# A new head, a middle without rstd and one weight unit split by hand in a decoder layer kernel

## The chip, the cores and the metric

One Trainium2 chip, one of its cores. The metric is the device time of one execution in microseconds (us). The core has the engines TensorE (PE), VectorE (DVE), ScalarE (ACT), GpSimd (POOL) and SyncE (SP); in this kernel SP issues the weight transfers and waits for nothing else that matters here.

## The reference

One layer of a decoder on x (256 rows of 1024 channels, float32), cut to what the kernel's parts need:

```
h   = rmsnorm(x, norm_mix)
o_a, o_b, o_c = attention mixers on columns of h @ w_in      # dilated, sparse, block-sparse
g   = sigmoid(the last 3 * 1024 columns of h @ w_in)          # one gate per branch and channel
merged = g0 * (o_a @ wb[:r0]) + g1 * (o_b @ wb[r0:r1]) + g2 * (o_c @ wb[r1:])
x   = x + merged @ w_out
a,u = split(causal_conv3(rmsnorm(x, norm_ffn) @ w_up) + conv_b)   # 2 * 2816 columns
x   = x + (silu(a) * u) @ w_down
out = rmsnorm(x, norm_final)       # rmsnorm(y, w) = y * rsqrt(mean(y*y) + 1e-6) * w
```

The convolution is depthwise over the 256 rows: for each channel, `w2 * y[t] + w1 * y[t-1] + w0 * y[t-2]`.

## The kernel before

Every weight matrix is stored as units, most of them 128x2048 float32 (1 MB). SP's queue loads a unit into a `raw` tile; ACT copies it to `whi`, rounded to the type that PE multiplies at its full rate (L225), and DVE takes the rest, `wlo = raw - whi` (L229), each in two halves of 128x1024. `raw`, `whi` and `wlo` sit in rings of five slots. An activation is split likewise (`hn_hi`, `hn_lo`; `mh`, `ml`; `fh`, `fl`), and a product is three matmuls into one PSUM tile: whi·lo, wlo·hi and whi·hi (`mm3`, L241 to L243; the weight is named first here). PE, ACT, DVE and POOL each run their own instructions in order; a scheduler sets that order, except inside a `manual_schedule` block, where it is the order of the code. The stages:

- Head. rstd of x's rows (ACT square L170, DVE L177/L179, POOL power L181), x scaled by it (L282, L290, L291), eight transposes per row tile through an identity matrix that came by DMA in `small_a` (L275), then parts hi (L302, L304) and lo (L307) with the norm weights as a per-partition scale. Idle matmuls (`keep_busy`, L262) fill PE. The first unit `a0` is multiplied chunk by chunk in the order of L337: hi·hi, lo·hi, hi·wlo; the next unit is `a1`.
- Projections and attention, up to 161 us, untouched by the change.
- Merge, four rounds `i` of two chunks `c`. A chunk has 24 products `g` with unit `br{i}` (three branches), DVE gates and adds them (`mg`: L713, L715 `tmp`, L716), ACT and DVE split the sum (`mh` L719, `ml` L720), and 12 matmuls of 128x512 with unit `wo{i}` go into four `acc` tiles. `later` holds these 12 back by a chunk or two; `flush` emits the last 24 of them. In round 1 `wlo` of the `br` unit is made on POOL instead of DVE (L697).
- Middle. x gets the residual (`add`, L735), then its rstd (`square`, POOL power), is scaled by rstd and by `norm_ffn` in one DVE instruction (`scale`, L742), transposed (`turned`, L748), split (`turn_hi` L752, `turn_lo` L756); four idle matmuls stand ahead (L774).
- MLP, 11 iterations of units `fa`, `fu`, `fd`, two channel chunks each. A chunk is 24 products with `fa`, 24 with `fu`, and 12 `acc` matmuls with `fd`. `conv` reads the PSUM tile three times: ACT L800, then DVE L802 twice; silu on ACT (L822), the product `sa` (L824), the split `fh` (L827) and `fl` (L828) follow.
- Final norm and store.

Of the kernel before, what the change touches and what calls it, by code (L numbers as in the profile page):

```python
# [32 lines left out]
A_ID, A_GM, A_N = 0, 128, 136  # L33
# [4 lines left out]
def _constants():  # L38
# [27 lines left out]
    return np.eye(P, dtype=np.float32), sel, mk, onehot, mask  # L66
# [36 lines left out]
def _laid_out(a):  # L103
# [3 lines left out]
    for name, src, rows, cols in _unit_list():  # L107
# [7 lines left out]
    eye, sel, mk, onehot, mask = _constants()  # L115
# [3 lines left out]
    small_a = np.concatenate([eye, turn(a["norm_mix"])], 1)  # L119
# [3 lines left out]
    return dict(x=a["x"][0], small_a=small_a, small_b=small_b, table=table, w1=w1, wts=wts,  # L123
                norms=np.stack([a["norm_ffn"][0], a["norm_final"]]))
# [3 lines left out]
def decoder_layer(ctx: ExitStack, tc, x, small_a, small_b, table, w1, wts, norms, out):  # L128
# [11 lines left out]
    xs = act_pool.tile([P, NT, D], F32, name="xs")  # L140
    sa_ = const.tile([P, A_N], F32, name="small_a")
# [8 lines left out]
    ident, g_mix = sa_[:, A_ID:A_ID + P], sa_[:, A_GM:A_GM + KC]  # L150
# [119 lines left out]
    u_a0 = Unit("a0", cuts=2)  # L270
    HALF = [slice(n * 512, (n + 1) * 512) for n in range(2)]
# [5 lines left out]
    with tc.manual_schedule(engines={mybir.EngineType.Activation, mybir.EngineType.DVE, mybir.EngineType.Pool,  # L277
                                     mybir.EngineType.PE}):
        keep_busy(WARM)
        r = rstd_of([square_mean(xs[:, 0, :], xn[0], "m0")], "m0")  # L280
        for sl in HALF:
            nc.vector.tensor_scalar_mul(xn[0][:, sl], xs[:, 0, sl], r)  # L282
        turn(0)
        keep_busy(2)
# [13 lines left out]
        u_a0.lo(0, 2, nc.gpsimd)  # L298
# [65 lines left out]
    for i in range(3):  # L364
# [4 lines left out]
        else:  # L369
            u = unit(f"a{i}")  # L370
# [313 lines left out]
    def flush(t):  # L684
        for n in range(2):
            for e in waiting:
                e(t, n)
        if t == NT - 1:
            waiting.clear()
# [43 lines left out]
    xn = [act_pool.tile([P, D], F32, name=f"xn{t}") for t in range(NT)]  # L733
# [3 lines left out]
    def square(t, n):  # L737
        return square_mean(xs[:, t, HALF[n]], xn[t][:, HALF[n]], f"f{t}{n}")

    def scale(t, r, n):  # L740
        for sl in HALF[n:n + 1]:
            nc.vector.scalar_tensor_tensor(xn[t][:, sl], xs[:, t, sl], r, g_ffn[:, sl], op0=ALU.mult, op1=ALU.mult)  # L742

    def turned(t, n):
        pool, name = ((psg, "g"), (psg2, "g"), (psa, "acc00"), (psa, "acc01"))[2 * t + n]
        ps = pool.tile([P, 512], F32, name=name).rearrange("p (c q) -> p c q", c=4)
        for c in range(4):
            nc.tensor.transpose(ps[:, c, :], xn[t][:, (4 * n + c) * P:(4 * n + c + 1) * P], ident)  # L748
        return ps

    def turn_hi(t, n, ps):
        nc.scalar.activation(h_hi[:, 4 * n:4 * n + 4, t * P:(t + 1) * P], ps, AF.Copy)  # L752

    def turn_lo(t, n, ps):
        hi = h_hi[:, 4 * n:4 * n + 4, t * P:(t + 1) * P]
        nc.vector.tensor_sub(h_lo[:, 4 * n:4 * n + 4, t * P:(t + 1) * P], ps, hi.bitcast(F32))  # L756

    fu = dict(first)
    with tc.manual_schedule(engines={mybir.EngineType.Activation, mybir.EngineType.DVE, mybir.EngineType.Pool}):
        flush(0)  # L760
        flush(1)
        add(0, 0)
        s00 = square(0, 0)
        add(0, 1)
        s01 = square(0, 1)
# [103 lines left out]
```

## Time and profile before

| what | value |
|---|---|
| three timed executions | 445.3, 445.21, 443.75 us, median 445.21 us |
| the profiled execution, its own time | 445.4 us |
| its span, first to last instruction | 443.6 us |
| mean granted TensorE clock | 0.991 |
| busy PE / DVE / ACT / POOL | 97% / 67% / 54% / 4% |

The span leaves 1.8 us of the execution's time to what lies around it. A busy time is the part of the span in which an engine had at least one instruction at work. The granted clock is a share of PE's full clock: 1.0 is 2.4 GHz, 0.5 is 1.2 GHz.

### The profile page before, as it was taken

Reading aid. Unit: us, or ns where it says so; the run is one execution under the profiler, and the core shown is the slowest. Engines: PE = TensorE matmul, PEld = TensorE weight load, DVE = VectorE, ACT = ScalarE, POOL = GpSimd, SP = SyncE. Lnnn points to the kernel's source line nnn. Section 1 sums busy time; section 2 is a strip of 40 time slices with the busy share of each in tenths; the row PEclk is TensorE's granted clock in tenths of the full one; section 3 lists DMA queues with packets and bytes.
Section 4 is the critical chain, followed back from the end, with each engine's and each line's share of the span. In section 5 each row is a group of like instructions: output and inputs, shape, how many; then the busy total and the mean of one; then the engine's idle time right before and its main releaser. Section 6 shows DMA issues by size and latency. Waiting matters only on the chain.

```text
span 443.6 us, 7635 instructions
## 1 busy us (share of the span) xinstructions
PE 430.0 (97%) x3094; PEld 391.2 (88%) x3094; DVE 295.5 (67%) x593; ACT 240.3 (54%) x420; POOL 17.8 (4%) x20
## 2 busy tenths in 40 slices
PE   7999999999999998999999899999999999999993
PEld 6998877977789996999998799999999999999982
DVE  4846742888466487646535998785785785875744
ACT  4643362558676772445442795465564573574423
POOL 2401000000000031000000100000000000000001
PEclk9999999999999998999999999999999999999997
DMA  8978746331127795345550177743733734700002
GB/s 305 395 287 277 262 166 258 136 150 41 57 95 269 270 364 190 128 157 191 189 191 1 61 278 279 284 154 131 285 134 151 286 104 181 264 22 1 1 0 95
DMA packets 12898, 78.66 MB, mean 177 GB/s; under 512 B 1424, under 2 KB 1568, under 8 KB 4928
## 3 DMA queue, kind: packets, MB, share of 16 engines
q1 hardware_dynamic: 12144, 76.00, 45.9%
q0 software_dynamic: 576, 2.12, 1.7%
q8 instruction: 24, 0.39, 0.4%
q10 hardware_dynamic: 144, 0.07, 0.1%
q14 instruction: 10, 0.08, 0.1%
HBM read 77.11 MB, written 1.07 MB: 176 GB/s over the span
## 4 chain that ended last, share of the span: by engine, by line
PE 92%; DVE 3%; ACT 2%; issue 1%; DMA 1%; POOL 1%; POOLq 0%; DVEq 0%
PE g L243 21%; PE g L241 21%; PE g L242 21%; PE acc L241 6%; PE acc L242 6%; PE acc L243 6%; PE s L428 3%; PE o L460 2%; PE g L337 2%; PE t L439 2%; PE o L522 1%; DMA xs<-in_x_dram 1%; DVE mg L716 1%; PE s L337 1%; ACT whi L225 0%
## 5 line engine op out<-in xcount | busy, mean ns | idle before, releaser
L229 DVE TENSOR_TENSOR wlo<-raw,whi 128x1024 fp32r<-128x1024 f32 (+2 forms) x132 | 151.5, 1177 | 54.8 <-ACT whi L225 53.7
L241 PE MATMUL g<-hn_hi,wlo 128*128 128x256 f32 x648 | 185.1, 286 | 0.0
L242 PE MATMUL g<-hn_lo,whi 128*128 128x256 f32 x648 | 184.4, 285 | 0.0
L243 PE MATMUL g<-hn_hi,whi 128*128 128x256 f32 x648 | 184.4, 285 | 0.0
L225 ACT ACTIVATE whi<-raw 128x1024 fp32r<-128x1024 f32 (+2 forms) x136 | 131.9, 1014 | 28.6 <-PE g L243 17.1
L241 PEld LDWEIGHTS g<-hn_hi,wlo 128*128 128x128 f32 x648 | 124.1, 192 | 3.8 <-issue 2.3
L242 PEld LDWEIGHTS g<-hn_lo,whi 128*128 128x128 f32 x648 | 124.1, 192 | 2.7 <-issue 1.9
L243 PEld LDWEIGHTS g<-hn_hi,whi 128*128 128x128 f32 x648 | 124.1, 192 | 1.3 <-issue 1.3
L802 DVE SCALAR_TENSOR_TENSOR cy<-g,small_b,cy 128x255 f32<-128x255 f32 (+1 forms) x88 | 42.0, 481 | 26.5 <-ACT cy L800 25.3
L800 ACT ACTIVATE cy<-g,small_b 128x256 f32<-128x256 f32 x44 | 24.8, 566 | 23.8 <-PE g L243 22.4
L241 PE MATMUL acc<-whi,fl 128*128 128x512 f32 x88 | 34.5, 393 | 0.0
L242 PE MATMUL acc<-wlo,fh 128*128 128x512 f32 x88 | 34.5, 392 | 0.0
L243 PE MATMUL acc<-whi,fh 128*128 128x512 f32 x88 | 34.3, 389 | 0.0
L827 ACT ACTIVATE fh<-sa 128x256 fp32r<-128x256 f32 x22 | 9.2, 417 | 34.7 <-DVE sa L824 34.7
L639 ACT ACTIVATE gl<-g 128x256 f32<-128x256 f32 x24 | 9.1, 381 | 23.6 <-PE g L243 23.6
L243 PEld LDWEIGHTS acc<-whi,fh 128*128 128x128 f32 x88 | 16.5, 188 | 3.6
L241 PEld LDWEIGHTS acc<-whi,fl 128*128 128x128 f32 x88 | 16.6, 189 | 3.0
L242 PEld LDWEIGHTS acc<-wlo,fh 128*128 128x128 f32 x88 | 16.6, 189 | 2.8
L242 PE MATMUL g<-o_lo,whi 128*128 128x256 f32 x64 | 18.1, 283 | 0.0
L243 PE MATMUL g<-o_hi,whi 128*128 128x256 f32 x64 | 18.1, 283 | 0.0
L241 PE MATMUL g<-o_hi,wlo 128*128 128x256 f32 x64 | 18.1, 283 | 0.0
L476 ACT ACTIVATE tt<-tt,nm 128x128 f32<-128x128 f32 (+1 forms) x32 | 14.3, 448 | 4.9 <-DVE nm L474 4.8
(176 smaller groups left out, 490.4 us busy)
## 6 DMA issues: line engine op xcount, KB each, us to landing
raw<-in_wts_dram SPq DMA_DIRECT2D x62, 1024.0 KB, 4.8
gl<-in_w_dram SPq DMA_DIRECT2D x8, 512.0 KB, 6.7
raw<-in_wts_dram SPq DMA_DIRECT2D x2, 804.0 KB, 8.0
raw<-in_wts_dram SPq DMA_DIRECT2D x3, 512.0 KB, 6.9
T<-tvd POOLq DMA_DIRECT2D x1, 1280.0 KB, 12.9
xs<-in_x_dram SPq DMA_DIRECT2D x2, 512.0 KB, 4.3
g<-in_norms_dram SPq DMA_DIRECT2D x2, 512.0 KB, 4.0
out_dram<-raw SPq DMA_DIRECT2D x4, 256.0 KB, 2.2
```

Of the source, the lines that this page charges most:

```text
L225: nc.scalar.activation(self.parts[0][:, sl], self.raw[:, sl], AF.Copy)
L229: (eng or nc.vector).tensor_sub(self.parts[1][:, sl], self.raw[:, sl], self.parts[0][:, sl].bitcast(F32))
L241: nc.tensor.matmul(ps, al, bh, start=start, stop=False)
L242: nc.tensor.matmul(ps, ah, bl, start=False, stop=False)
L243: nc.tensor.matmul(ps, ah, bh, start=False, stop=stop)
L337: nc.tensor.matmul(ps, view(a, k), b[:, k, :], start=(a == 0 and b is h_hi and k == 0), stop=(a == 1 and k == KC - 1))
L428: nc.tensor.matmul(pss[i][:, o], q[rows, q0:q0 + P], k[rows, 0:k1], start=True, stop=True)
L476: nc.scalar.activation(t[:, a:b], t[:, a:b], AF.Exp, bias=nm[:, i:i + 1], accum_out=z[:, i:i + 1])
L639: nc.scalar.activation(gl[c][:, b, :], chunk_T(plain(u, c)), AF.Copy)
L800: nc.scalar.activation(y, ps, AF.Identity, bias=vec_c[:, 3, ch:ch + 1], scale=vec_c[:, 2, ch:ch + 1])
L802: nc.vector.scalar_tensor_tensor(y[:, sh:], ps[:, :S - sh], vec_c[:, w, ch:ch + 1], y[:, sh:], op0=ALU.mult, op1=ALU.add)
L827: nc.scalar.activation(fh, sa, AF.Copy)
```

## The change

Four parts. (1) The head makes the identity on POOL, finds `norm_mix` and `norm_ffn` as eight further columns of x's rows, takes 16 idle matmuls of 128x128 in place of six of 128x256 and drops the later ones, computes both rstd before any scaling, shares the scaling and the split of `a0` differently, splits `a1` by hand, and orders the products of the first chunk hi·hi, then by halves of k. (2) `wlo` of `br1` is made on DVE. (3) In the middle x is transposed as it is, and `norm_ffn` enters in the split; the products of `fa0` and `fu0` are written out by hand with `fu0` split between them; rstd comes later, as a row (`rows`, two small fp32 matmuls). The idle matmuls go. (4) `conv` multiplies the PSUM tile by `rows` on DVE first (`u`) and works on `u` in SBUF. The core of the diff:

```
-WARM = 6
+WARM = 16
...
-    nc.scalar.dma_start(sa_, small_a)
+    g_mix, g_ffn = xs[:, 0, D:D + KC], xs[:, 1, D:D + KC]
...
+    nc.gpsimd.affine_select(out=ident, in_=idle, compare_op=ALU.not_equal, fill=1.0, base=0, pattern=[[-1, P]],
+                            channel_multiplier=1)
...
-        keep_busy(WARM)
-        r = rstd_of([square_mean(xs[:, 0, :], xn[0], "m0")], "m0")
-        for sl in HALF:
-            nc.vector.tensor_scalar_mul(xn[0][:, sl], xs[:, 0, sl], r)
-        turn(0)
-        keep_busy(2)
...
+        for _ in range(WARM):
+            nc.tensor.matmul(pt[:, :P], idle, idle, start=True, stop=True)
+        r0 = rstd_of([square_mean(xs[:, 0, 0:D], xn[0], "m0")], "m0")
...
+        scaled(0, 0, r0, "v")
+        scaled(0, 1, r0, "a")
+        turn(0)
+        scaled(1, 0, r1, "v")
+        scaled(1, 1, r1, "a")
         turn(1)
-        u_a0.hi(0, 2)
-        keep_busy(1)
...
+        split_hi(0, "v")
+        split_hi(1, "a")
+        u_a0.lo(0, 2, nc.gpsimd)
+        for c in (0, 1):
+            hi_part(c, "v")
+        for c in (2, 3):
+            hi_part(c, "a")
+        split_hi(2, "a")
+        split_hi(3, "a")
+        u_a0.lo(1, 2, nc.gpsimd)
+        for c in range(4, KC):
+            hi_part(c, "v")
+        for i in range(2):
+            u_a1.hi(i, 2)
+        for c in range(KC):
             lo_part(c)
+        for i in range(2):
+            u_a1.lo(i, 2)
...
-        u = unit(f"br{i}", eng=nc.gpsimd if i == 1 else None)
+        u = unit(f"br{i}")
...
+def turn_hi(c):
+        nc.scalar.activation(h_hi[:, c, :], xT[c], AF.Copy, scale=g_ffn[:, c:c + 1])
...
+        for t in range(NT):
+            flush(t, 0)
+            add(t, 0)
+            sq[t, 0] = square(t, 0)
+        flush(0, 1)
         add(0, 1)
+        xT += turned(0)
+        flush(1, 1)
...
+        split_x(0)
         add(1, 1)
+        split_x(2)
+        first_products(0, h_hi, range(4))
+        u_f.lo(0, 2)
+        xT += turned(1)
+        first_products(0, h_lo, range(4))
+        split_x(4)
+        split_x(6)
+        first_products(0, h_hi, range(4, KC))
+        u_f.lo(1, 2)
+        for t in range(NT):
+            sq[t, 1] = square(t, 1)
+        rs = [rstd_of([sq[t, 0], sq[t, 1]], f"f{t}") for t in range(NT)]
+        fu["fa1"] = unit("fa1")
+        first_products(0, h_lo, range(4, KC))
+
+        rp = psa.tile([P, 512], F32, name="acc00")[:, :S]
+        for t in range(NT):
+            nc.tensor.matmul(rp[:, t * P:(t + 1) * P], rs[t].to_broadcast([P, P]), ident, start=True, stop=True)
+        nc.scalar.activation(rows, rp, AF.Copy)
...
-        nc.scalar.activation(y, ps, AF.Identity, bias=vec_c[:, 3, ch:ch + 1], scale=vec_c[:, 2, ch:ch + 1])
+        u = scaled.pop(0)
+        scaled.append(u)
+        nc.vector.tensor_mul(u, ps, rows)
+        nc.scalar.activation(y, u, AF.Identity, bias=vec_c[:, 3, ch:ch + 1], scale=vec_c[:, 2, ch:ch + 1])
         for w, sh in ((1, 1), (0, 2)):
-            nc.vector.scalar_tensor_tensor(y[:, sh:], ps[:, :S - sh], vec_c[:, w, ch:ch + 1], y[:, sh:],
+            nc.vector.scalar_tensor_tensor(y[:, sh:], u[:, :S - sh], vec_c[:, w, ch:ch + 1], y[:, sh:],
```

`split_x(c0)` makes the hi parts of two chunks of x on ACT and then their lo parts on DVE; `first_products(part, b, ks)` multiplies one part of both units by one part of x into four PSUM tiles. The lines of the diff move instructions on the queues; three places follow.

DVE in the first merge round, before. `mg_1956` is the gated sum of round 0, chunk 0, `mg_1995` that of chunk 1, `ml_1991` the lo part that the first 12 `acc` matmuls need, and `wlo_2227` belongs to unit `wo1`.

```order
L713 TENSOR_TENSOR mg_1956<-g_1958,gl_1549 128x256
L715 TENSOR_TENSOR tmp_1957<-g_1969,gl_1549 128x256
L716 TENSOR_TENSOR mg_1956<-mg_1956,tmp_1957 128x256
L715 TENSOR_TENSOR tmp_1957<-g_1981,gl_1549 128x256
L716 TENSOR_TENSOR mg_1956<-mg_1956,tmp_1957 128x256
L713 TENSOR_TENSOR mg_1995<-g_1997,gl_1550 128x256
L720 TENSOR_TENSOR ml_1991<-mg_1956,mh_1990 128x256
```

The same place after the change; `mg_1967`, `mg_2006` and `ml_2002` are the same three, `wlo_2058` is `br1`'s lo part, `wlo_2238` that of `wo1`.

```order
L725 TENSOR_TENSOR mg_1967<-g_1969,gl_1560 128x256
L227 TENSOR_TENSOR wlo_2058<-raw_2056,whi_2057 128x1024
L727 TENSOR_TENSOR tmp_1968<-g_1980,gl_1560 128x256
L227 TENSOR_TENSOR wlo_2058<-raw_2056,whi_2057 128x1024
L728 TENSOR_TENSOR mg_1967<-mg_1967,tmp_1968 128x256
L725 TENSOR_TENSOR mg_2006<-g_2008,gl_1561 128x256
L727 TENSOR_TENSOR tmp_1968<-g_1992,gl_1560 128x256
L727 TENSOR_TENSOR tmp_2007<-g_2019,gl_1561 128x256
L728 TENSOR_TENSOR mg_1967<-mg_1967,tmp_1968 128x256
L728 TENSOR_TENSOR mg_2006<-mg_2006,tmp_2007 128x256
L727 TENSOR_TENSOR tmp_2007<-g_2031,gl_1561 128x256
L227 TENSOR_TENSOR wlo_2238<-raw_2236,whi_2237 128x1024
L732 TENSOR_TENSOR ml_2002<-mg_1967,mh_2001 128x256
```

Two halves of `br1` moved in among chunk 0's adds, a half of `wo1` moved ahead of `ml`, and `ml` comes after the multiplications of chunk 1.

PE at the same place, before: the last product of chunk 1 (`g_2020`) and the first `acc` matmuls.

```order
L241 MATMUL g_2020<-o_hi_84,wlo_1941 128x256
L242 MATMUL g_2020<-o_lo_85,whi_1940 128x256
L243 MATMUL g_2020<-o_hi_84,whi_1940 128x256
L241 MATMUL acc00_1935<-whi_1948,ml_1991 128x512
L242 MATMUL acc00_1935<-wlo_1949,mh_1990 128x512
L243 MATMUL acc00_1935<-whi_1948,mh_1990 128x512
```

After, the last rows before the first `acc` matmul; `g_2098` is the third branch of round 1, chunk 0.

```order
L239 MATMUL g_2098<-o_hi_83,wlo_2058 128x256
L240 MATMUL g_2098<-o_lo_84,whi_2057 128x256
L241 MATMUL g_2098<-o_hi_83,whi_2057 128x256
L239 MATMUL g_2098<-o_hi_83,wlo_2058 128x256
L240 MATMUL g_2098<-o_lo_84,whi_2057 128x256
L239 MATMUL acc00_1946<-whi_1959,ml_2002 128x512
```

23 of the 24 products of round 1, chunk 0 (`g_2075`, `g_2086`, `g_2098`) moved ahead of the first 12 `acc` matmuls; the 24th stands right behind them, and the 12 of chunk 1 follow at once.

PE in the middle, before, from the last `acc` matmul of the merge to the MLP's third batch of products.

```order
L243 MATMUL acc_1938<-whi,mh 128x512
L774 MATMUL acc_2805<-small_a 128x128 x4
L748 MATMUL g<-small_a,xn_2761 128x128 x8
L748 MATMUL acc_2830<-small_a,xn_2762 128x128 x4
L748 MATMUL acc_2835<-small_a,xn_2762 128x128 x4
L337 MATMUL g<-hn_hi,whi 128x256 x16
L337 MATMUL g<-hn_lo,whi 128x256 x16
L337 MATMUL g<-hn_hi,wlo 128x256 x16
```

After, from the last `acc` matmul; ahead of it the first eight transposes stand between `acc` matmuls of the flush, with six of those behind them.

```order
L241 MATMUL acc_1949<-whi,mh 128x512
L781 MATMUL g<-hn_hi,whi 128x256 x16
L760 MATMUL acc_2853<-ident,xs 128x128 x4
L760 MATMUL acc_2854<-ident,xs 128x128 x4
L781 MATMUL g<-hn_lo,whi 128x256 x16
L781 MATMUL g<-hn_hi,whi 128x256 x16
L781 MATMUL g<-hn_lo,whi 128x256 x16
L822 MATMUL acc_2940<-ident,rsf_2910 128x128
L822 MATMUL acc_2940<-ident,rsf_2914 128x128
L827 MATMUL g<-hn_hi,wlo 128x256 x32
```

The transposes now read `xs` and no scaled copy, products stand between the two groups of them, and the two matmuls with rstd (`rsf`) stand behind 64 products.

## Rows read from the trace of the kernel before

**Rows 1.** The page: its first line, and the busy time of each engine.

```profile
span 443.6 us, 7635 instructions
PE 430.0 (97%) x3094; PEld 391.2 (88%) x3094; DVE 295.5 (67%) x593; ACT 240.3 (54%) x420; POOL 17.8 (4%) x20
```

**Rows 2.** PE's waits: who waited for whom, us in total, times, longest.

```profile
PE acc L241 <- DVE ml L720: 1.9, 1, 1.9
...
PE g L748 <- DVE xn L742: 0.9, 2, 0.6
PE acc L748 <- DVE xn L742: 0.5, 1, 0.5
```

**Rows 3.** The timeline of the head: start, duration, engine, instruction, [idle before, released by].

```profile
1.10 4.98 PE L262 MATMUL g<-tt 128*128 128x256 f32 x12 [1.10 <-POOL tt L257]
...
9.63 0.66 PE L275 MATMUL t<-small_a,xn 128*128 128x128 f32 x4 [0.50 <-DVE xn L290]
...
10.11 0.88 DVE L302 TENSOR_SCALAR hn_hi<-t,small_a 128x256 fp32r<-128x256 f32 x2 [0.54 <-PE t L275]
...
11.94 1.66 DVE L307 SCALAR_TENSOR_TENSOR hn_lo<-t,small_a,hn_hi 128x256 fp32r<-128x256 f32 x4
...
15.08 5.02 DVE L229 TENSOR_TENSOR wlo<-raw,whi 128x1024 fp32r<-128x1024 f32 x4
...
17.87 0.39 PE L241 MATMUL g<-hn_hi,wlo 128*128 128x256 f32 x1
```

**Rows 4.** The timeline of the merge's first round.

```profile
162.54 4.94 POOL L229 TENSOR_TENSOR wlo<-raw,whi 128x1024 fp32r<-128x1024 f32 x2 [122.71 <-ACT whi L225]
...
163.23 0.43 DVE L715 TENSOR_TENSOR tmp<-g,gl 128x256 f32<-128x256 f32 x1 [0.66 <-PE g L243]
...
163.69 1.55 DVE L716 TENSOR_TENSOR mg<-mg,tmp 128x256 f32<-128x256 f32 x1
...
165.80 1.96 DVE L716 TENSOR_TENSOR mg<-mg,tmp 128x256 f32<-128x256 f32 x1
...
168.12 1.99 ACT L225 ACTIVATE whi<-raw 128x1024 fp32r<-128x1024 f32 x2
...
168.72 0.50 PE L241 MATMUL acc<-whi,ml 128*128 128x512 f32 x1 [1.94 <-DVE ml L720]
...
169.04 0.42 DVE L716 TENSOR_TENSOR mg<-mg,tmp 128x256 f32<-128x256 f32 x1
...
173.16 0.28 PE L241 MATMUL g<-o_hi,wlo 128*128 128x256 f32 x1
```

**Rows 5.** Windows: us, busy PE, PEld, DVE, ACT, POOL (instructions), clock, DMA share, GB/s.

```profile
170.00:171.00 1.00, 1.00 (x4) 0.71 (x4) 0.97 (x2) 0.53 (x2) 0.00 (x0) 0.50 1.00 426
...
245.20:249.30 4.10, 2.62 (x17) 1.68 (x17) 3.53 (x7) 2.39 (x5) 0.99 (x1) 1.00 0.00 0
249.30:260.90 11.60, 11.60 (x96) 11.60 (x97) 11.22 (x17) 11.52 (x18) 0.00 (x0) 1.00 0.66 239
320.54:337.54 17.00, 17.00 (x122) 16.02 (x121) 12.32 (x18) 9.63 (x14) 0.00 (x0) 1.00 0.50 188
```

**Rows 6.** The timeline of the middle.

```profile
243.23 0.39 PE L243 MATMUL acc<-whi,mh 128*128 128x512 f32 x1
...
243.91 0.40 PE L243 MATMUL acc<-whi,mh 128*128 128x512 f32 x1
...
244.15 1.05 PE L774 MATMUL acc<-small_a 128*128 128x128 f32 x8
...
247.96 1.32 PE L748 MATMUL acc<-small_a,xn 128*128 128x128 f32 x8 [0.55 <-DVE xn L742]
...
250.89 4.63 DVE L229 TENSOR_TENSOR wlo<-raw,whi 128x1024 fp32r<-128x1024 f32 x4
```

**Rows 7.** The timeline of DVE in one iteration of the MLP.

```profile
326.96 1.00 DVE L802 SCALAR_TENSOR_TENSOR cy<-g,small_b,cy 128x255 f32<-128x255 f32 x2
...
334.36 0.42 DVE L828 TENSOR_TENSOR fl<-sa,fh 128x256 fp32r<-128x256 f32 x1 [0.48 <-ACT fh L827]
```

More of the change, by code (lines that the diff above doesn't have):

```diff
@@ L253, in decoder_layer @@
     ps_o = mixer.enter_context(tc.tile_pool(name="ps_o", bufs=2, space=bass.MemoryType.PSUM))
-    idle = att.tile([P, 384], F32, name="tt", bufs=3)[:, :S]
+    idle = att.tile([P, 384], F32, name="tt", bufs=3)[:, :P]
     nc.gpsimd.memset(idle, 0.0)
+    nc.gpsimd.affine_select(out=ident, in_=idle, compare_op=ALU.not_equal, fill=1.0, base=0, pattern=[[-1, P]],
+                            channel_multiplier=1)
     pt = psg.tile([P, 512], F32, name="g")
-    def keep_busy(n):
-        for _ in range(n):
-            nc.tensor.matmul(pt[:, :S], idle[:, :P], idle, start=True, stop=True)
     h_hi, h_lo = normed_tiles()
@@ L682, in later, with flush @@
                     e(t, n)
[L684 to L689, printed above, removed]
+    def flush(t, n):
+        for e in waiting:
+            e(t, n)
     branch_k = ((0, 3), (3, 6), (6, 8))
@@ L732, in decoder_layer @@
     h_hi, h_lo = normed_tiles()
-    xn = [act_pool.tile([P, D], F32, name=f"xn{t}") for t in range(NT)]
+    spare = [act_pool.tile([P, D], F32, name=f"xn{t}") for t in range(NT)]
+    rows, scaled = spare[1][:, 0:S], [spare[1][:, i * S:(i + 1) * S] for i in range(1, 4)]
+    HALF = [slice(n * 512, (n + 1) * 512) for n in range(2)]
     def add(t, n):
@@ L751, in turn_hi @@
[L751 to L756, printed above, removed]
-    fu = dict(first)
[L759 to L763, printed above, removed]
-        add(0, 1)
-        s01 = square(0, 1)
-        add(1, 0)
-        s10 = square(1, 0)
-        r = rstd_of([s00, s01], "f0")
-        add(1, 1)
-        s11 = square(1, 1)
-        ps = psa.tile([P, 512], F32, name="acc10")
-        for _ in range(4):
-            nc.tensor.matmul(ps[:, :P], ident, ident, start=True, stop=True)
-        scale(0, r, 0)
-        tp = [turned(0, 0)]
-        r1 = rstd_of([s10, s11], "f1")
-        scale(0, r, 1)
-        tp.append(turned(0, 1))
-        for n in range(2):
-            turn_hi(0, n, tp[n])
-        scale(1, r1, 0)
-        scale(1, r1, 1)
-        tp += [turned(1, n) for n in range(2)]
-        for n in range(2):
-            turn_lo(0, n, tp[n])
-            turn_hi(1, n, tp[2 + n])
-        for n in range(2):
-            turn_lo(1, n, tp[2 + n])
-        for name in ("fu0", "fd0"):
-            fu[name] = unit(name)
@@ new lines, in square, with turned @@
+        return square_mean(xs[:, t, HALF[n]], spare[0][:, HALF[n]], f"f{t}{n}")
+    def turned(n):
+        pss = [psa.tile([P, 512], F32, name=f"acc{t}{n}").rearrange("p (c q) -> p c q", c=2) for t in range(NT)]
+        for c in range(4):
+            for t in range(NT):
+                nc.tensor.transpose(pss[c // 2][:, c % 2, t * P:(t + 1) * P],
+                                    xs[:, t, (4 * n + c) * P:(4 * n + c + 1) * P], ident)
+        return [pss[c // 2][:, c % 2, :] for c in range(4)]
@@ new lines, in decoder_layer, with turn_lo, first_products @@
+    xT = []
+    def turn_hi(c):
+        nc.scalar.activation(h_hi[:, c, :], xT[c], AF.Copy, scale=g_ffn[:, c:c + 1])
+    def turn_lo(c):
+        nc.vector.scalar_tensor_tensor(h_lo[:, c, :], xT[c], g_ffn[:, c:c + 1], h_hi[:, c, :].bitcast(F32),
+                                       op0=ALU.mult, op1=ALU.subtract)
+    fu = dict(first)
+    firsts = [gtile() for _ in range(4)]
+    def first_products(part, b, ks):
+        for k in ks:
+            for i in range(2):
+                for j, u in enumerate((fu["fa0"], fu["fu0"])):
+                    nc.tensor.matmul(firsts[2 * i + j], u[part][:, k, i * P:(i + 1) * P], b[:, k, :],
+                                     start=b is h_hi and k == 0, stop=False)
@@ L794, in decoder_layer @@
+    waiting.clear()
     merge.close()
```

105 lines of the change are left out of this document (53 added, 52 removed).

## The prediction

> **What bounds the kernel now.** I read the page's first lines, then PE's waits, then the timelines of the three places that these point to, and windows for the clock. PE is busy 430.0 of 443.6 us [rows 1], so time is won only where PE stands still, runs at half clock, or does work that can go. After the head PE's list of waits has two places [rows 2]: one wait of 1.9 us in the merge and three, 1.4 us together, for the scaled x in the middle; the reader is to see that the 22 chunks of the MLP add none. The profiled execution took 445.4 us with a span of 443.6, so 1.8 us lie around it; my sum is made against 445.4, which is 0.2 above the median of 445.21.
>
> **Head.** Before, 12 idle passes of 256 columns take 4.98 us, 0.415 each [rows 3]. Sixteen fp32 matmuls are 32 passes of 128 columns; at half of that, 0.21 each, they end near 7.8 us, about where row tile 0 is ready. The second tile's transposes start at 9.63 before; with its square ahead of the first tile's scaling on DVE (0.88) they can start near 8.7, and DVE's first hi part, 0.48 after them as now (9.63 to 10.11), comes at 9.18. But DVE then has six hi parts at 0.44 and eight lo parts at 0.415 [rows 3]: 9.18 + 2.64 + 3.32 = 15.14. There it begins `wlo` of a1, which it begins at 15.08 now. The second half of a1 is done at 15.14 + 2 x 1.255 = 17.65, and PE's first matmul that needs it runs at 17.87 now. So PE may finish a0 1.5 us earlier and wait for a1 instead. I take **+0.1 us** of gain, between -0.7 (idle matmuls at the full 0.415 per pass push everything back) and +0.6.
>
> **Merge.** POOL's two halves of `br1` take 4.94 us from 162.54 [rows 4]. While they run, DVE's adds with both operands in SBUF (L716) take 1.55 and 1.96 us; after them the same add takes 0.42, and L715, which reads one operand from PSUM, takes 0.43 even beside POOL. That makes `ml` late, PE waits 1.94, and then PE runs at half clock: 0.50 in the window from 170 [rows 5]. From the end of the last product, about 166.6, to the next product at 173.16 are 6.53 us for 12 matmuls that take 0.227 each at full clock ((243.91 - 243.23) / 3, [rows 6]), 2.73 in all. The loss is 3.8 us.
>
> After, POOL is idle here and DVE does the two halves, 2 x 1.16 ([rows 6]: 4.63 for four). They fit between 162.5 and 165.4, while PE still has products up to 166.6, so `br1` is ready for the 23 products that now follow: 23 x 0.121 (11.60 / 96, [rows 5]) = 2.8, to 169.4. What is late next is `ml`: on ACT a half of `wo1` (1.0, half of 1.99) stands ahead of `mh` and waits for the products' end at 166.6; it ends at 167.7, `mh` (0.42) at 168.2; on DVE a half of `wo1` stands ahead of `ml`, and `ml` is ready between 169.5 and 170.05. PE waits 0.1 to 0.65 us. Behind `ml` on DVE stand the adds of chunk 1, whose 12 matmuls come 2.7 us later: enough. Waits of 0.5 in the middle left the clock at 1.00 [rows 5], so I keep full clock. Gain **3.1 us**, between 2.5 (a wait of 1.3) and 3.8 (none).
>
> **Middle.** From the last `acc` matmul (244.15) to the first product (249.30) PE takes 5.15 us, and the transposes in it are 16 x 0.165 = 2.64 [rows 6]. After, no rstd, power or scaling stands between the sum and the transposes, the first eight lie inside the flush and the others between products. The idle matmuls (1.05 us, inside the waits) go. Two fp32 matmuls of 128x128 come: eight passes for four took 1.05, so 0.52. All else of PE's work stays. Gain 5.15 - 2.64 - 0.52 = 2.0, if nothing new waits. The removed load of `norm_ffn` and the one moved early are covered by idle queues; SP has nothing of this stage behind them.
>
> Something new may wait, on DVE. It is 97% busy from 249.3 to 260.9 already [rows 5], and gets a multiplication per product tile (`u`). Let the flush end where it does before, with its first eight transposes: 245.5. By the rows' durations x's last lo part is done near 251.0. Up to the first `fl` DVE then has seven halves of `wlo` (8.1), four multiplications (0.43 each as L715, 1.7), eight convolution steps (0.48 each, 3.8; [rows 7] give 1.00 for two), and 1.25 of small ones: 14.9, so 265.9, or 266.8 with waits for ACT. PE arrives at its first `fl` after 96 + 55 products: 245.5 + 1.3 + 0.5 + 151 x 0.121 = 265.6. So it waits 0.3 to 1.2 there, and perhaps as long once more at the fourth chunk, before DVE has caught up. I take 1.0 for the sum of these waits, W, between 0 and 2.5. Net gain of the middle **+1.0 to 1.1**.
>
> The Trainium skill ("VectorE: DVE Perf Modes", the table of instruction costs) gives a VectorE instruction a smaller fixed cost from SBUF, 58 cycles, than from PSUM, 120. By it the eight convolution steps that now read `u` from SBUF would each save 65 ns and W would be 0.5 us less, an estimate. The rows here show no such difference: L716 with both operands in SBUF takes 0.42 beside 0.43 for L715 with one in PSUM [rows 4].
>
> **MLP.** The last of the window cuts is where a chunk's `acc` matmuls start. DVE is busy 12.32 of 17.0 us of an iteration [rows 5]; four multiplications at 0.42 make 14.0, 82%. `fl` ends at 334.78 [rows 7], and PE takes it at 337.54, 2.76 later. The chain of a chunk grows by one or two multiplications and what DVE puts between, up to 1.6: hidden, at nothing. If that cover were gone, each microsecond beyond 2.76 would be paid per iteration. In the last chain the one multiplication, 0.42, stands beside PE's last deferred `acc` matmuls: nothing.
>
> **Sum.** 445.4 - 0.1 - 3.1 - 1.1 = 441.1; less 0.1 for the profiled execution's distance to the median, **441.0 us**.
>
> **Rivals.**
> *All waits vanish (0.10).* DVE keeps up after the middle and the head gains 0.6: 445.4 - 0.6 - 3.4 - 2.0 = 439.3. For it: a chunk's 2.76 us of slack. Against it: the 14.9 us above.
> *The clock falls in the head (0.10).* Between about 7.5 and 9.9 us PE now runs only transposes, with gaps. In the merge the half clock after 1.94 us of idleness cost 4.44 - 2.73 = 1.7 us (168.72 to 173.16, [rows 4]). The same here would be mostly covered, because a1's `wlo` sets 17.65 anyway: up to 0.5 of it is paid, 441.5. Against it: from 245.2 to 249.3 PE ran nothing but transposes, with four waits, at a clock of 1.00 [rows 5]. The Trainium skill ("TensorE: Matmul & The Clock Gate", Part 4) says that transposes don't count as PE-busy in the same way, which would bring the fall; the trace's 1.00 speaks against it.
> *The backlog eats the middle (0.12).* W is 2.5 and the longest wait brings the half clock with its 1.7: 445.4 - 0.1 - 3.1 + 2.2 = 444.4, no change.
> *The merge keeps its stall (0.08).* DVE's halves of `br1` wait for ACT's, `ml` slips by 2 us more, PE idles as before and falls to half clock: 445.4 - 0.1 - 1.1 = 444.2, no change.
> *DVE becomes the bound of the MLP (0.08).* At 82% DVE is the next engine, and its order puts `wlo` halves (1.16) between the links of a chunk's chain. From a delay beyond 2.76 us on, PE waits in every iteration. Three halves and the two multiplications more, 4.3 - 0.8 for gaps, are 3.5: 0.75 x 10 iterations = 7.5 lost, 441.0 + 7.5 = 448.5. For it: the ring of five slots lets `wlo` run ahead whenever a load lands. Against it: 3 us of DVE's 17 stay free.
>
> **How the numbers follow.** The forecast with its own bounds (439.5 to 442.5) gets 0.52. From the bounds of the terms together with the two cases near 444.3 the range is 438.6 to 444.4; it leaves out the slower case and little below. A measurement of this kernel can tell about 0.5%, 2.2 us, from no change: faster means below 443.0. Forecast, no waits and clock in the head give 0.72 with some of the backlog's lighter forms; the two cases near 444 give 0.20, and 0.08 is slower.
>
> **What would show it.** Right: PE's list without a wait of 1.9 for `ml`, L728 at 0.42, the clock at 1.00 from 166 to 173; no gap of PE between the flush and the MLP's products, and the MLP's iterations some 4 us ahead of now; a1's fourth matmul at 17.7; waits for `fl` of 0.5 to 2 us near 263, and none later; DVE at some 75%. Wrong: a fall of the clock in any of these places, waits for `fl` or for PSUM tiles that the multiplications free late, repeated every 17 us, or PE waiting for a `wlo` of the middle's units.

## The result and the profile after

The change makes the kernel faster: 441.25 us, median of five executions (440.2 to 442.03), beside 443.86 us for five of the kernel before (443.73 to 445.3). The ratio is 0.9915, with a 95% interval of 0.9893 to 0.9938. The profiled execution of after took 441.25 us with a span of 439.4, so the span is 4.2 us shorter than that of [rows 1]. The sum of the forecast, 4.3 us off the profiled execution, is met almost exactly. Its terms are not.

The medians lie closer together, 2.6 us, than the two spans. The kernel before was timed in 41 executions beside this kernel and the experiments: 20 took 445.2 us or more, 19 took 443.65 to 444.25, and two lie between. Where the mean granted clock is known, it is 0.988 to 0.994 in the first group and 0.994 to 0.998 in the second. So the fall to half clock that the trace of before shows in the merge seems to come in about half of its executions, for some 1.6 us. The forecast was added up from an execution with it (445.4, clock 0.991); of the five above, three took 443.73 to 443.86.

The page of after, its first line and the busy times:

```profile
span 439.4 us, 7725 instructions
PE 428.6 (98%) x3104; PEld 392.2 (89%) x3104; DVE 307.0 (70%) x637; ACT 241.6 (55%) x421; POOL 16.3 (4%) x19
```

PE's waits of after answer to [rows 2]. The 1.9 us for `ml` and the three waits for the scaled x are gone; one new line of that size stands in their place, 2.1 us for the rstd that GpSimd makes.

```profile
PE acc L822 <- POOL rsf L179: 2.1, 1, 2.1
PE g L284 <- POOL tt L255: 1.0, 1, 1.0
PE t L273 <- DVE xn L279: 0.3, 1, 0.3
```

To find where the time went, one takes the same event of the program in both traces and subtracts. Three such events of the kernel before: the first gating of the merge, the first of the last 36 `acc` matmuls of the merge, and the first addition behind the MLP.

```profile
162.15 0.42 DVE L713 TENSOR_TENSOR mg<-g,gl 128x256 f32<-128x256 f32 x1 [0.53 <-PE g L243]
...
235.95 0.40 PE L241 MATMUL acc<-whi,ml 128*128 128x512 f32 x1
...
430.55 0.69 DVE L728 TENSOR_TENSOR xs<-acc,xs 128x512 f32<-128x512 f32 x1 [1.82 <-PE acc L243]
```

The same three in the kernel after:

```profile
160.53 0.42 DVE L725 TENSOR_TENSOR mg<-g,gl 128x256 f32<-128x256 f32 x1 [0.49 <-PE g L241]
...
230.80 0.40 PE L239 MATMUL acc<-whi,ml 128*128 128x512 f32 x1
...
426.23 0.69 DVE L740 TENSOR_TENSOR xs<-acc,xs 128x512 f32<-128x512 f32 x1 [1.31 <-PE acc L241]
```

The differences are 1.62, 5.15 and 4.32 us. So up to the merge 1.62 us are won, in the merge 5.15 - 1.62 = 3.53, and between there and the end of the MLP 0.83 are lost again:

| stage | forecast, gain | measured, gain |
|---|---|---|
| head | 0.1 | 1.6 |
| merge | 3.1 | 3.5 |
| middle and MLP | 1.1 | -0.8 |
| sum | 4.3 | 4.3 (4.2 of the span) |

Both traces hold one fall of the clock, before in the merge and after in the middle, so the 3.5 contains what the fall cost before and the -0.8 what it costs after.

In the middle of after, VectorE's three subtractions begin in the same moment as GpSimd's two powers, and PE waits at L822 until the first power is done:

```profile
246.69 3.50 DVE L227 TENSOR_TENSOR wlo<-raw,whi 128x1024 fp32r<-128x1024 f32 x3
246.74 4.39 POOL L179 TENSOR_TENSOR rsf<-msf,half 128x1 f32<-128x1 f32 x2 [211.66 <-DVE msf L177]
...
250.65 1.32 PE L822 MATMUL acc<-ident,rsf 128*128 128x128 f32 x4 [2.07 <-POOL rsf L179]
251.63 5.28 PE L827 MATMUL g<-hn_hi,wlo 128*128 128x256 f32 x32
```

The two powers apart, as the view of the tile `rsf` gives them (shortest, median and longest in ns), and the windows behind the wait (columns as in [rows 5]):

```profile
L179 POOL TENSOR_TENSOR rsf<-msf,half x2: 545/2200/3855, 246.7 to 250.6; 128x1 f32<-128x1 f32 x2
```

```profile
250.00:252.00 2.00, 1.34 (x6) 1.12 (x7) 0.18 (x1) 0.00 (x0) 1.13 (x2) 0.74 0.99 410
252.00:254.00 2.00, 2.00 (x11) 2.00 (x11) 0.21 (x1) 1.99 (x3) 0.00 (x0) 0.50 1.00 406
```

The first power, on 128 numbers, takes 3.86 us and the second 0.55. VectorE's chain ends at 250.19 and the first power 0.4 us later, at 250.60. After the wait PE runs at 0.50 for a while, as it did in the merge before.

The trace of the kernel before held this price already. There two powers met one VectorE instruction each that reads two operands from SBUF, the first in the middle and the second at the end of the kernel:

```profile
245.96 0.74 DVE L742 SCALAR_TENSOR_TENSOR xn<-xs,rsf,g 128x512 f32<-128x512 f32 x1
246.12 0.99 POOL L181 TENSOR_TENSOR rsf<-msf,half 128x1 f32<-128x1 f32 x1 [1.69 <-DVE msf L179]
...
434.24 0.68 DVE L838 TENSOR_TENSOR raw<-xs,g 128x512 f32<-128x512 f32 x1
434.40 0.93 POOL L181 TENSOR_TENSOR rsz<-msz,half 128x1 f32<-128x1 f32 x1 [187.29 <-DVE msz L179]
```

Both end 0.41 us after VectorE's instruction (246.70 and 434.92), and take 0.99 and 0.93 us; with VectorE idle the same instruction takes 0.55 to 0.56 there (at 6.01 and 8.50).

### The profile page after: what moved, and what is told of

Its sections match the earlier page's. It is cut to its first block, busy times and chain, and to the rows that moved or that the text cites. A ratio compares the mean times of both kernels' runs of the same rounds, so it can differ in the third digit from the quotient of the medians.

```text
span 439.4 us, 7725 instructions
## 1 busy us (share of the span) xinstructions
PE 428.6 (98%) x3104; PEld 392.2 (89%) x3104; DVE 307.0 (70%) x637; ACT 241.6 (55%) x421; POOL 16.3 (4%) x19
## 4 chain that ended last, share of the span: by engine, by line
PE 91%; DVE 2%; issue 2%; POOL 2%; DMA 1%; ACT 1%; POOLq 0%; SPq 0%
PE g L241 21%; PE g L239 21%; PE g L240 21%; PE acc L239 6%; PE acc L240 6%; PE acc L241 6%; PE s L443 3%; PE o L475 2%; PE t L454 2%; DMA raw<-in_wts_dram 1%; PE g L827 1%; PE o L537 1%; POOL rsf L179 1%; POOL wlo L227 1%; DVE hn_lo L770 1%
## 5 line engine op out<-in xcount | busy, mean ns | idle before, releaser
L239 PE MATMUL g<-hn_hi,wlo 128*128 128x256 f32 x632 | 180.7, 286 | 0.0
L241 PE MATMUL g<-hn_hi,whi 128*128 128x256 f32 x632 | 179.9, 285 | 0.0
L240 PE MATMUL g<-hn_lo,whi 128*128 128x256 f32 x632 | 179.9, 285 | 0.0
L223 ACT ACTIVATE whi<-raw 128x1024 fp32r<-128x1024 f32 (+2 forms) x130 | 129.6, 1039 | 40.8 <-PE g L241 28.4
L239 PEld LDWEIGHTS g<-hn_hi,wlo 128*128 128x128 f32 x632 | 121.1, 192 | 3.8 <-issue 2.3
L240 PEld LDWEIGHTS g<-hn_lo,whi 128*128 128x128 f32 x632 | 121.1, 192 | 2.7 <-issue 1.9
L241 PEld LDWEIGHTS g<-hn_hi,whi 128*128 128x128 f32 x632 | 121.1, 192 | 1.4 <-issue 1.3
L844 DVE SCALAR_TENSOR_TENSOR cy<-xn,small_b,cy 128x255 f32<-128x255 f32 (+1 forms) x88 | 41.8, 481 | 11.4 <-ACT cy L842 10.4
L842 ACT ACTIVATE cy<-xn,small_b 128x256 f32<-128x256 f32 x44 | 26.0, 596 | 17.2 <-DVE xn L841 17.2
L841 DVE TENSOR_TENSOR xn<-g,xn 128x256 f32<-128x256 f32 x44 | 18.5, 422 | 13.2 <-PE g L241 9.6
```

What stands on the lines that cost most here:

```text
L223: nc.scalar.activation(self.parts[0][:, sl], self.raw[:, sl], AF.Copy)
L239: nc.tensor.matmul(ps, al, bh, start=start, stop=False)
L240: nc.tensor.matmul(ps, ah, bl, start=False, stop=False)
L241: nc.tensor.matmul(ps, ah, bh, start=False, stop=stop)
L841: nc.vector.tensor_mul(u, ps, rows)
L842: nc.scalar.activation(y, u, AF.Identity, bias=vec_c[:, 3, ch:ch + 1], scale=vec_c[:, 2, ch:ch + 1])
```

## The experiments

The theory after the result: **GpSimd and VectorE keep each other out when both read two operands from SBUF.** That made `ml` late in the merge before, and in the middle of after it makes the power late. The rival for the middle: the first power after some 200 us of idleness of GpSimd is slow by itself. The power at 434.40 above, 0.93 us after 187 us of idleness, speaks against it; e3 tests it. Each ratio is to the kernel before, timed beside that run; spans are of one profiled execution each.

| run | span, us | median, us (n) | lowest to highest | ratio to before, 95% interval |
|---|---|---|---|---|
| after | 439.4 | 441.25 (5) | 440.2 to 442.03 | 0.9915, 0.9893 to 0.9938 |
| e1, merge only | 440.1 | 441.91 (4) | 441.81 to 442.21 | 0.9941, 0.9918 to 0.9964 |
| e2, head only | 440.9 | 443.74 (10) | 441.97 to 445.31 | 0.997, 0.9948 to 0.9991 |
| e3, power alone | 436.1 | 438.08 (4) | 437.65 to 438.58 | 0.9855, 0.983 to 0.9879 |
| e4, rstd row later | 437.6 | 439.39 (4) | 438.77 to 439.58 | 0.988, 0.9852 to 0.9909 |
| e5, wait filled | 438.4 | 440.25 (4) | 440.2 to 441.0 | 0.9901, 0.9873 to 0.993 |
| e6, `br1` on GpSimd again | 441.5 | 442.43 (9) | 441.49 to 445.2 | 0.9957, 0.9931 to 0.9983 |
| e7, square late | 440.2 | 441.95 (1) | | |
| e8, small load | 438.2 | 439.96 (1) | | |
| e9, after again | 439.6 | 441.24 (4) | 439.7 to 441.41 | 0.9899, 0.9857 to 0.9942 |
| e10, e3 again | 436.1 | 437.89 (6) | 437.71 to 440.01 | 0.9845, 0.9814 to 0.9876 |

**e1, the merge alone.** The kernel before, with

```
-        u = unit(f"br{i}", eng=nc.gpsimd if i == 1 else None)
+        u = unit(f"br{i}")
```

> The kernel before with one edit: the lo part of br1 is made on VectorE instead of GpSimd; head, middle and MLP as before. Theory (GpSimd's subtraction slows VectorE's adds with both operands in SBUF, and that makes ml late): the wait of 1.9 us for ml and the stretch at clock 0.50 go, the adds take 0.42 us, and the time falls by 3.4 to 3.8 us (span about 440.0). Rival (the merge was short of VectorE time anyway, the stall only moves behind VectorE's two more halves): a wait of 1 us or more for ml stays, with the half clock, and the time moves by less than 1 us.

The span is 440.1, 3.5 us less, as the theory has it. That is against the profiled execution of before, with its fall of the clock; against the executions of before near 443.8 the median of e1 gains 1.9. The list of PE's waits has no line for `ml`. The adds between the two halves of `br1` and behind them take 0.42 each, and `ml` ends at 169.56, inside the forecast's 169.5 to 170.05 (e1 has the head of before, so its times compare directly):

```profile
164.03 1.22 DVE L229 TENSOR_TENSOR wlo<-raw,whi 128x1024 fp32r<-128x1024 f32 x1
165.16 0.42 DVE L716 TENSOR_TENSOR mg<-mg,tmp 128x256 f32<-128x256 f32 x1
...
169.14 0.42 DVE L720 TENSOR_TENSOR ml<-mg,mh 128x256 fp32r<-128x256 f32 x1
```

**e6, the other way round.** The changed kernel, with that line as it was before.

> The changed kernel with the lo part of br1 back on GpSimd. Theory (GpSimd and VectorE slow each other here, in the new order of the head and the middle as in the old): VectorE's adds with both operands in SBUF take 1.5 to 2 us beside GpSimd, PE waits 1.9 to 2.3 us for ml, and the span rises from 439.4 to 441.7 without a fall of the clock behind the wait, to 443.3 with one. Rival (the 3.5 us came from the order of PE's rows, 23 products ahead of the first acc matmuls, and the scheduler keeps it): no wait, span 439.4.

The stall is back in the new surroundings: two slow adds, a wait of 1.96 us, and half clock behind it.

```profile
161.99 1.58 DVE L728 TENSOR_TENSOR mg<-mg,tmp 128x256 f32<-128x256 f32 x1
...
164.13 1.96 DVE L728 TENSOR_TENSOR mg<-mg,tmp 128x256 f32<-128x256 f32 x1
...
167.05 0.50 PE L239 MATMUL acc<-whi,ml 128*128 128x512 f32 x1 [1.96 <-DVE ml L732]
```

The span rises by 2.1 us only, where the same events count 234.28 - 230.80 = 3.5 up to the last 36 `acc` matmuls of the merge. The difference is the clock of the middle: PE waits 2.1 us for `rsf` again, but the window behind it reads 1.00, where after has 0.50:

```profile
254.00:256.00 2.00, 1.83 (x13) 1.64 (x14) 0.00 (x0) 0.82 (x2) 0.60 (x2) 1.00 1.04 430
```

From that event to the first addition behind the MLP e6 takes 194.0 us, after 195.4 and before 194.6. So the middle as it stands wins 0.6 us where the clock holds and loses 0.8 where it falls. The other runs agree: 194.0 in e8 (clock 1.00), 195.3 and 195.5 in e9 and e7 (half clock).

**e2, the head alone.** The kernel before with part 1 of the change, the first chunk of the MLP in its old order.

> The kernel before with the new head alone; merge, middle and MLP as before, the first chunk of the MLP in its old order. Theory (the trace after is read rightly: the fourth matmul of a1 comes at 16.17 us instead of 17.87, and nothing behind gives it back): the time falls by 1.5 to 1.7 us (span about 442.0). Rival (what the forecast said, the lo part of a1 holds the end of the head at 17.65): 0.1 us. Second rival (the attention stage, which waits on loads, takes it back): less than 0.5 us.

The span fell by 2.7 us, more than expected, but not all of it is the head's. The fourth matmul of a1, the first of its second step in k, comes at 16.43, 1.44 us earlier than the 17.87 of [rows 3]; that part agrees with the theory and not with 0.1. The rest is the clock: PE waits 2.3 us for `ml` here, and runs on at full clock.

```profile
PE acc L239 <- DVE ml L743: 2.3, 1, 2.3
```

```profile
170.00:171.00 1.00, 1.00 (x8) 0.88 (x7) 1.00 (x2) 0.00 (x0) 0.00 (x0) 1.00 0.63 262
```

The same window of the kernel before, the first of [rows 5], has 0.50. So the fall of the clock behind such a wait is not there in every execution, and a span of one execution holds it or not. The medians, 443.74 for e2 and 444.81 for the kernel before beside it, differ by 1.1 us.

**e3, the power alone.** The changed kernel, and one more instruction on VectorE:

```
         rs = [rstd_of([sq[t, 0], sq[t, 1]], f"f{t}") for t in range(NT)]
+        nc.vector.tensor_copy(spare[0][:, 0:1], rs[1])
         fu["fa1"] = unit("fa1")
```

> The changed kernel with one instruction more: VectorE copies one column of the second rstd into scratch before it splits fa1, so that it stands still until GpSimd's two powers are done (one half of another unit still lies ahead of the copy). Theory A (GpSimd's power crawls while VectorE subtracts with both operands in SBUF): the first power takes at most 1.7 us instead of 3.86, the second 0.55, PE's wait for rsf falls from 2.07 to below 0.3 us, the clock stays 1.00 from 248 to 258, and the span falls from 439.4 to 436.7, or 437.5 if VectorE's own delay makes an fl late. Theory B (the first power after some 200 us of idleness of GpSimd is slow by itself, by its code's loading for one): it takes 3.9 us again, PE waits 2.0, span 439.4 to 440.2.

Theory A holds, its rival is refuted: the idleness is the same and the power is not slow. One half of another unit still runs beside the first power, which ends at 248.32, again 0.4 us after VectorE's subtraction (247.92). The second runs with VectorE standing still and takes 0.54.

```profile
246.70 1.22 DVE L227 TENSOR_TENSOR wlo<-raw,whi 128x1024 fp32r<-128x1024 f32 x1
246.74 2.12 POOL L179 TENSOR_TENSOR rsf<-msf,half 128x1 f32<-128x1 f32 x2 [209.96 <-DVE msf L177]
...
248.42 0.98 PE L823 MATMUL acc<-ident,rsf 128*128 128x128 f32 x4
...
249.16 4.08 PE L828 MATMUL g<-hn_hi,wlo 128*128 128x256 f32 x32
```

GpSimd had been idle for 210 us, as in after, and its first power took 1.58 us instead of 3.86. PE's wait is gone, the clock is 1.00 from 248 to 260, and the span falls to 436.1, 3.3 us below after and 0.6 below the expectation. Counted between the same two events as above, the middle and the MLP take 192.1 us in e3, and in e10 too, so the 3.3 us are 1.9 for the wait (194.0 in e6 and e8) and 1.4 for the half clock behind it (195.4 in after). One instruction more makes the kernel faster than before and after.

```profile
230.80 0.40 PE L239 MATMUL acc<-whi,ml 128*128 128x512 f32 x1
...
422.87 0.69 DVE L740 TENSOR_TENSOR xs<-acc,xs 128x512 f32<-128x512 f32 x1 [1.32 <-PE acc L241]
```

**e10** is the same kernel timed in more rounds.

> The changed kernel with the one VectorE copy that makes it stand aside for GpSimd's powers, timed in more rounds. Theory (no PE wait of more than 0.3 us is left behind the head, so neither the wait nor a fall of the clock is paid): median 437.6 to 438.6, spread below 1 us, a ratio of about 0.985 to the kernel before; the wait for rsf stays absent in the trace. Rival (the first look was a lucky one): a spread like that of the changed kernel, and single executions above 439.5.

The ratio to before is 0.9845, with an interval from 0.9814 to 0.9876, which overlaps that of after timed beside it (e9, 0.9857 to 0.9942). The times themselves are further apart: the medians are 437.89 and 441.24, and only one execution of e10 is above the lowest of e9, 439.7. Five of six executions lie between 437.71 and 438.75; one at 440.01, at a granted clock of 0.998, lies outside what the theory allowed, and its cause stays open.

**e4, the rstd row later.** The changed kernel, with the two small matmuls behind 24 of the 32 products that need no rstd:

```
+        for i in range(3):
+            last_products(i)
         rp = psa.tile([P, 512], F32, name="acc00")[:, :S]
...
         nc.scalar.activation(rows, rp, AF.Copy)
+        last_products(3)
```

> The changed kernel with the two small matmuls for the rstd row moved behind 24 of the 32 products that need no rstd. The power stays as slow as it is. Theory (the 2.07 us wait and the half clock after it cost 2.9 us only because of the place where PE meets the power): no wait for rsf, clock 1.00 throughout, span 436.5 to 437.0. Rival (the PSUM tiles of the four first products are held until the row is there, and the next products wait for a tile): a new wait of 1 to 2 us of PE's products for VectorE's multiplication, span 438 to 439.4.

The rival came true: the wait for `rsf` is gone, and 1.4 us of waiting stand at the next products, for a PSUM tile that VectorE's multiplication holds. The multiplication stands behind two halves of `wlo` on VectorE:

```profile
251.95 2.36 DVE L227 TENSOR_TENSOR wlo<-raw,whi 128x1024 fp32r<-128x1024 f32 x2 [1.38 <-issue]
...
254.23 0.42 DVE L845 TENSOR_TENSOR xn<-g,xn 128x256 f32<-128x256 f32 x1
...
254.70 0.39 PE L239 MATMUL g<-hn_hi,wlo 128*128 128x256 f32 x1 [1.44 <-DVE xn L845]
```

So moving PE's part does not do what freeing the power does; e4 is 1.5 us behind e3.

**e5, the wait filled.** The changed kernel, with eight idle matmuls ahead of L822:

```
+        for _ in range(8):
+            nc.tensor.matmul(rp[:, :P], ident, ident, start=True, stop=True)
```

> The changed kernel with eight idle fp32 matmuls of 128x128 on PE ahead of the two that make the rstd row, about as long as the wait of 2.07 us (eight passes took 1.05 us before). The power stays slow, and PE meets it at the same time. Theory (of the 3.5 us that the middle loses against its sum of work, 2.07 are the wait and 1.5 the half clock behind it, 0.98 instead of 0.52 for the two matmuls and 4.93 instead of 3.84 for the 32 products): the clock stays 1.00 from 248 to 258 and the span falls from 439.4 to 437.9. Rival (the half clock has another cause than PE's idleness, or is not worth anything because VectorE is late behind it): span 439.2 to 439.6.

The clock stays at 1.00 and the span is 438.4, half a microsecond above the expectation. e8 below shows what this is worth: there the same wait of 2.07 us was not filled, the clock stayed at 1.00 too, and the span was 438.2. e8's window behind the wait:

```profile
252.00:254.00 2.00, 2.00 (x20) 2.00 (x18) 1.05 (x2) 2.00 (x3) 0.00 (x0) 1.00 0.93 385
```

So the half clock, where it comes, costs about 1.2 to 1.4 us (439.4 and 439.6 against 438.2), not 1.5, and the wait costs the rest of the 3.3 that e3 wins. One profiled execution does not show that the idle matmuls kept the clock up. The four timed ones (440.2 to 441.0, clock 0.994 to 0.995) are all shorter than six of the nine of after and e9, which took 441.2 or more at 0.991 to 0.993. That speaks for it, but four are few.

**e7, the square late.** The changed kernel, with VectorE's square of the second row tile behind its scaling of the first, as before.

> The changed kernel with VectorE's square of the second row tile moved behind its scaling of the first, as in the kernel before. Theory (the head won because the second rstd comes early): the second tile's transposes start 0.5 to 0.9 us later than 7.99, the lo part of a1 begins at 14.4 to 14.8 instead of 13.93, and the fourth matmul of a1 comes at 16.5 to 17.0 instead of 16.17. Rival (the head is set by the landing of the first half of a0, which the split waits for at 8.10): both move by 0.3 us at most.

For the head of after, the lines to compare with:

```profile
7.99 0.60 PE L273 MATMUL t<-ident,xn 128*128 128x128 f32 x4
8.10 0.43 DVE L304 CAST whi<-raw 128x512 fp32r<-128x512 f32 x1 [0.60 <-DMA raw<-in_wts_dram]
...
8.81 4.77 POOL L227 TENSOR_TENSOR wlo<-raw,whi 128x1024 fp32r<-128x1024 f32 x2 [1.06 <-ACT whi L306]
8.98 0.39 PE L352 MATMUL g<-hn_hi,whi 128*128 128x256 f32 x1
...
13.93 2.35 DVE L227 TENSOR_TENSOR wlo<-raw,whi 128x1024 fp32r<-128x1024 f32 x2
...
16.17 0.39 PE L239 MATMUL g<-hn_hi,wlo 128*128 128x256 f32 x1
```

And of e7:

```profile
8.64 0.66 PE L273 MATMUL t<-ident,xn 128*128 128x128 f32 x4 [0.38 <-DVE xn L279]
...
14.61 2.35 DVE L227 TENSOR_TENSOR wlo<-raw,whi 128x1024 fp32r<-128x1024 f32 x2
...
16.79 0.39 PE L239 MATMUL g<-hn_hi,wlo 128*128 128x256 f32 x1
```

The transposes come 0.65 us later, the lo part of a1 0.68, the matmul 0.62, as the theory said. The size is less sure than these figures look: in the seven executions profiled with the head of after (after, e3 to e6, e9, e10) the matmul comes between 16.09 and 16.53. So the early second rstd is worth 0.3 to 0.7 us of the head's gain. The rest, about a microsecond, is not taken apart by a run. By the trace it is the split of `a0`: its first quarters start on two engines as soon as they land, at 8.10, where the kernel before started the first half on ACT behind the scaling, so that GpSimd began its subtraction at 8.81 instead of 10.83. That is argued, not shown.

**e8, a small load.** The changed kernel with a load of the removed one's size on ScalarE's queue, its data unused.

> The changed kernel with a load of 128x136 float32 on ScalarE's queue at the start, of the size of the one that the change removed; what it loads is not used. Theory (without that load x lands earlier: the first square begins at 4.05 us instead of 4.60, and the first half of a0 is there at 8.10): the first square begins 0.3 to 0.6 us later and the fourth matmul of a1 0.2 to 0.6 us later than 16.17. Rival (x's loads do not feel 70 KB more): the first square at 4.05, the fourth matmul of a1 at 16.2.

Half right: the first square begins 0.43 us later than after's 4.05 (3.98 to 4.16 in the seven executions with this head), and the matmul of a1 stays within their 16.09 to 16.53.

```profile
4.48 1.06 ACT L168 ACTIVATE xn<-xs 128x1024 f32<-128x1024 f32 x1 [1.81 <-DMA xs<-in_x_dram]
...
16.18 0.38 PE L239 MATMUL g<-hn_hi,wlo 128*128 128x256 f32 x1
```

x does land later with the load, but the first part of a0 still lands at 8.1, and the delay is covered by it. Taking the load out won nothing by itself that these executions can tell.

**e9, after once more.**

> The changed kernel as it is, once more. Theory (the fall of the clock behind a PE wait of some 2 us comes in some executions and not in others, and is worth some 1.2 to 1.8 us): the wait for rsf is 2.07 us again; the profiled span is either near 439.4 with 0.50 from 252 to 254, or near 438.2 with 1.00; the timed executions spread over 1.3 us or more, between 440.0 and 442.2. Rival (the clock falls whenever PE has waited this long, and the runs without a fall differed in something else): 0.50 again, span 439.4, and a spread below 0.8 us.

The fall came again, with the span at 439.6:

```profile
252.00:254.00 2.00, 2.00 (x11) 2.00 (x11) 0.00 (x0) 1.64 (x3) 0.00 (x0) 0.50 0.96 406
```

The timed executions spread over 1.7 us, one at 439.7 and three between 441.2 and 441.41. In the five executions of after the mean granted clocks 0.991, 0.993 and 0.993 go with 441.25, 442.03 and 441.29 us, and 0.996 twice with 440.61 and 440.2. That is what a fall in some executions would give, and the kernel before shows the same with more of them (20 against 19).

## Why the prediction was right, and where it was not

The forecast of 441.0 us beside 441.25 measured is right in its sum because the errors of the terms cancel: 1.5 us too little gain in the head and 0.4 in the merge against 1.9 too much in the middle. That is luck, and so is a second thing: the sum starts from an execution of before with the fall of the clock and meets a median of after that has one too. From the median of 443.86 the same gains would have given 439.6.

Two lines that the list needs: the first matmul that reads the second half of a1's `wlo`, in before, and the load of the first `ml` into PE in after, with PE's wait for it.

```profile
19.05 0.28 PE L241 MATMUL g<-hn_hi,wlo 128*128 128x256 f32 x1
```

```profile
167.91 0.19 PEld L239 LDWEIGHTS acc<-whi,ml 128*128 128x128 f32 x1 [0.19 <-DVE ml L732]
```

- **What bounds the kernel.** PE, as said; its busy share rose from 97% to 98%, and what was won are its waits and half clock.
- **Head, 0.1 forecast, 1.6 measured.** The step that failed is "PE's first matmul that needs it runs at 17.87": that row is the second step in k of a1, and the second half of `wlo` is first needed at the fifth, at 19.05 before. VectorE had finished it at 17.59, 1.46 us earlier. With that row read rightly the forecast's other figures would still have held PE by 0.4 us, at the first half of a1's `wlo` (15.14 + 1.255 = 16.40, needed 1.5 before 17.47), for a gain of 1.1. The second error covers this: VectorE began the lo part of a1 at 13.93, not 15.14. Its first hi part came at 8.45 instead of 9.18, and its 14 parts took 5.48 us instead of 5.96. So a1's lo part held nothing, and the 1.5 us by which I had PE finish a0 earlier came through whole.
- **Merge, 3.1 forecast, 3.5 measured.** The mechanism was right in both directions (e1, e6): the slow adds, `ml`, the wait, the clock. The term was mis-sized at the remaining wait, 0.1 to 0.65 us, taken near its upper end. It was near the lower one: PE's next matmul could have started at 167.76 and started at 167.91, with `ml` done at 167.86. What the prediction did not see is that the half clock in its 3.8 us of loss does not come in every execution. In e2, where the clock held behind the wait, the merge took 72.3 us between the events above, and 73.8 in before.
- **Middle, a gain of 1.1 forecast, a loss of 0.8 measured.** The PE work was right: with the power freed, e3 lies 4.0 us below e1, and 4.0 - 1.6 for the head leaves 2.4 for the middle (2.5 by the events, 194.6 - 192.1), beside the 2.0 of the forecast before its waits. What failed is "if nothing new waits", at a place I did not look: I had the price of GpSimd's instruction beside VectorE's in the merge, in [rows 4], and did not carry it over to the two powers. Before, they ran beside no such instruction of VectorE (0.56 us) and beside one (0.99); the change moved them to the start of three subtractions, where they took 4.39. The waits that I did forecast for `fl`, 1.0 us in sum, did not come in after, and in e3 only 0.24 of them: there PE could have taken the first `fl` at 260.87; it ends at 260.96, and PE takes it at 261.11. The fourth was ready in time, at 278.41 for 278.86.
- **MLP, nothing forecast, nothing measured.** VectorE is busy 13.72 of 17.0 us of an iteration, 14.0 forecast, and an `fl` ends 1.9 us before PE takes it (331.31 for 333.22); no wait is listed.
- **The rivals.** The fall of the clock in the head did not come: the granted clock of after reads 1.00 in every window from 6 to 13 us, transposes and gaps included. What did come is near "the backlog eats the middle" in its size, 2.1 us of waiting and a half clock, but by another mechanism. Two slips in the prediction's figures change nothing: "All waits vanish" adds up to 439.4, not 439.3, and PE's waits among the transposes from 245.2 to 249.3 are three, not four.

## What to carry to other kernels

Where GpSimd has even a tiny instruction on the path to PE, look at what VectorE runs in that moment: an instruction that reads two operands from SBUF is where the two keep each other out, and one copy that makes VectorE stand aside for a microsecond won 3.3 here, 1.9 of them the wait and 1.4 the half clock behind it. A price that a trace shows at one place, here the slow adds of the merge, is to be looked for at every place to which the change moves one of the two parties. A load or split "that must be ready by then" is to be dated by the first instruction that reads its second half, not by the first instruction of its consumer; and a total that comes out as forecast says little until the events in between are compared one by one.

## What was not expected of the hardware

GpSimd loses a whole chain, not one instruction. The power that met one subtraction took 1.58 us (e3, e10), the one that met three in a row 3.85 to 3.86 (after and e4 to e9), and in after and e3 it ended 0.4 us after the last of them; alone it took 0.54 to 0.56. In the merge it went the other way, and by single instructions: an add of VectorE that met a subtraction of GpSimd ended when that one instruction was over (at 165.24 and 167.76, GpSimd's halves ending near 164.9 and at 167.48). The Trainium skill ("SBUF — State Buffer", Who interferes with whom) says that VectorE with two SBUF inputs and GpSimd share a port pair, and that the one that comes first has it for the whole instruction while the other blocks. The merge agrees; in the middle the power also had to let pass two subtractions that began after it. Why it lost to them stays open.

The clock falls to 0.50 behind a PE wait of some 2 us in some executions and not in others: it fell behind 1.94 us before, 1.96 in e6 and 2.07 in after, e7 and e9, and did not fall behind 2.26 in e2, 2.07 in e8 and the 2.1 for `rsf` in e6. What decides it stays open. Kernels with such a wait spread over 1.6 to 3.9 us, e1, e3, e4 and e5 without it over 0.4 to 0.9; e10, with 2.3, does not fit.
